# 128 unused bytes in front of two groups of stationary tiles in a one-core decoder trunk

## The chip, the cores and the metric

The kernel runs on one core of one Trainium2 chip. The metric is the device time of one execution in microseconds (us). Three timed runs of the kernel before took 2246.64, 2246.13 and 2247.63 us; their median is 2246.64 us.

## The reference

One layer of a hybrid decoder on 256 tokens of width 2048, in float32:

```python
x = x + 0.5 * _swiglu(_rmsnorm(x, ffn1_norm[l]), ffn1_w_gu[l], ffn1_w_down[l])
x = x + _token_mixing(_rmsnorm(x, mix_norm[l]), w_in[l], ...)
x = x + 0.5 * _swiglu(_rmsnorm(x, ffn2_norm[l]), ffn2_w_gu[l], ffn2_w_down[l])
```

`_swiglu` is `(silu(gate) * up) @ w_down` with a hidden width of 5632. The token mixing projects the normalised input once to 10,788 columns, runs three attention mixers on parts of it, multiplies each mixer's output by a branch matrix (256, 512 and 768 rows) and by a sigmoid gate, adds the three, and multiplies the sum by `w_out` (2048 x 2048). Almost all of the arithmetic is in the large matrix products, whose weights (some 400 MB) are each used once.

## The kernel before, in words

**The weight stream.** Every large product goes through `add_chunk` (L148): 256 tokens in two blocks `tb` of 128, times a chunk of 512 columns of a weight matrix (384 or 420 in part of the input projection). The weights are the moving operand, the activations the stationary one. A chunk is cut into units of two row blocks of 128. The weights are loaded by SyncE's queue, four row blocks at a time, into one of three `raw` tiles (L101). ScalarE rounds a unit into a `hi` tile (L111) and VectorE takes the rest into a `lo` tile (L112); there are four tiles of each. Then TensorE runs, for each row block `kt` and each token block, three matmuls into one PSUM bank:

```python
PE.matmul(o, lhs(kt, 0, tb), hi[:, k], start=kt == 0, stop=False)
PE.matmul(o, lhs(kt, 0, tb), lo[:, k], start=False, stop=False)
PE.matmul(o, lhs(kt, 1, tb), hi[:, k], start=False, stop=kt == nkt - 1)
```

These are lines 162, 163 and 164. Each loads its own 128 x 128 stationary operand first (the weight load, engine row PEld), so the first two load the same one twice. A full unit has 12 such matmuls. The order of the work is written out by hand in `stream` (L127): splits run three units ahead of the matmuls.

**The stationary tiles.** The activations, too, are kept in two parts, transposed: a tile `[128, n, 2, 256]` of 4-byte elements holds for row block `kt`, part `p` and token block `tb` the slice `[:, kt, p, tb*128:(tb+1)*128]`, which is 128 elements, 512 bytes in each partition, without gaps. Four tiles have this form, and each large product has one of them as its stationary operand:

- `xT` (L61, 16 row blocks): the normalised residual; for all of the gate and up products of both feed-forward parts and for the input projection.
- `ffn_midt` (L243, 24 row blocks; printed for both feed-forward parts under one name): for the down products. Each feed-forward part runs in two halves (L238), the first with 24 row blocks, the second with 20, each followed by four chunks of down product.
- `oT` (L406, 12 row blocks): the attention outputs, for the branch products.
- `mT` (L921, 16 row blocks): the merged branches, for the output projection.

**Where the tiles lie.** `xT` belongs to the pool `per`, which stays open to the end. The other three belong to pools that are opened on top of `per` when they are needed and closed again: `ffn_midt` is the first tile of its pool, `oT` the first of the pool `mix`, and `mT` the first of the pool `merge`, which lies behind `oT`. Tiles of a pool follow one another in the order of the program, each rounded up to a multiple of 32 bytes. In one partition `xT` takes 32,768 bytes; behind it come three `raw` (8,192 each), four `hi` and four `lo` (4,096 each), `ident`, `rows` and `cols` (512 each) and `dump` (2,048), all multiples of 512; then small tiles: `ssq` 32, `mhalf` 64, three `rstd` 32 each, three tables of 1,024, 1,024 and 3,072, `tabcmp` 512, `tabq12` 64, `tabq8`, `sink`, `nsink` and `gain` 32 each, and `w2` 1,024. What isn't a multiple of 512 among them adds up to 32 + 64 + 96 + 64 + 128 = 384. So `ffn_midt` and `oT` begin 100,736 bytes behind the start of `xT`, which is 196 times 512 and 384 more, and `mT` begins 24,576 bytes (48 times 512) behind `oT`. All `raw`, `hi` and `lo` tiles begin at the same offset modulo 512 as `xT`. `ffn_midt` begins 67,968 bytes behind the end of `xT`.

**Around it.** After a unit's matmuls, TensorE also runs short work that other lines have spawned: transposes of activations (L219, L269, L479, L701, L718, L937) and the attention products.

Of the kernel before, what the change touches and what calls it, by code (L numbers as in the profile page):

```python
# [9 lines left out]
F32 = mybir.dt.float32  # L10
# [6 lines left out]
T, D, FF = 256, 2048, 5632  # L17
# [15 lines left out]
class Ring:  # L33
    """Buffers handed out and given back in emission order."""

# [11 lines left out]
def hybrid_trunk_kernel(ctx, tc, x, ffn1_norm, ffn1_w_gu, ffn1_w_down, mix_norm, w_in, qk_gain, sinks, cmp_pos,  # L47
# [6 lines left out]
    per = ctx.enter_context(tc.tile_pool(name="per", bufs=1))  # L54
# [19 lines left out]

# [1 line left out]
    chains = []  # L76
# [17 lines left out]
    def add_load(src, nk, width, parts):  # L94
        """src: [128, nk, width] in DRAM; parts: [(k0, nk, mm, before, after)]"""
        li = len(loads)
        loads.append((src, nk, width))
        for k0, n, mm, before, after in parts:
            subs.append((li, k0, n, width, mm, before, after))
# [5 lines left out]
    def emit_split(si, k=None):  # L105
        """split of a unit, or of its k-th slice of 128 rows"""
        li, k0, n, width, *_ = subs[si]
        c = slice(0, n * width) if k is None else slice(k * width, (k + 1) * width)
        raw = raws[li % RAW_BUFS][:, k0 * width:(k0 + n) * width][:, c]
        hi, lo = his[si % SPLIT_BUFS][:, c], los[si % SPLIT_BUFS][:, c]  # L110
        ACT.activation(hi, raw, AF.Copy)  # L111
        DVE.tensor_tensor(lo, raw, hi.bitcast(F32), op=OP.subtract)  # L112
# [35 lines left out]
    def add_chunk(w, rows0, nkt, c0, width, lhs, evac, before=None, between=()):  # L148
        """out[tok, c0:c0+width] = lhs^T @ w[rows0:rows0+128*nkt, c0:c0+width]; lhs(kt, part, tb) -> [128, 128]."""
        bank = main[2 * (chunk_no[0] % 2):][:2]  # L150
        chunk_no[0] += 1
        wv = w[rows0:rows0 + 128 * nkt, c0:c0 + width].rearrange("(k p) c -> p k c", p=128)

        def mm_of(kt0, n):
            def mm(hi, lo):
                ks = [(k, tb) for k in range(n) for tb in range(2)]
                if kt0 + n == nkt:
                    ks.sort(key=lambda a: a[1])
                for k, tb in ks:
                    kt = kt0 + k  # L160
                    o = bank[tb][:, :width]
# [3 lines that stand above are left out]
            return mm  # L165

        step = SPLIT_KT if not loads else LOAD_KT
        for l0 in range(0, nkt, step):
            ln = min(step, nkt - l0)
            parts = []  # L170
            for s0 in range(0, ln, SPLIT_KT):
                sn = min(SPLIT_KT, ln - s0)
                last = l0 + s0 + sn == nkt
                first = l0 + s0 == 0
                parts.append((s0, sn, mm_of(l0 + s0, sn), before if first else None,
                              (lambda: evac(bank)) if last else None))
            add_load(wv[:, l0:l0 + ln], ln, width, parts)
            for args in between[l0 // step:l0 // step + 1]:
                add_load(*args)
# [14 lines left out]

# [1 line left out]
    def x_squares(j):  # L196
# [9 lines left out]
    def x_prep(norm, j):  # L206
        """The norm's share of columns 512j.., and their transposed two-part copy with the gain."""
        g0 = GAIN_ROW[norm]
# [25 lines left out]

# [1 line left out]
    def add_ffn(norm, w_gu, w_down, done):  # L236
# [3 lines left out]
        def open_pools():  # L240
            st["ctx"] = es = ExitStack()
            p = es.enter_context(tc.tile_pool(name=f"{norm}_mid", bufs=1, reuse_waits="tile"))
            st["mid"] = p.tile([128, 24, 2, T], F32R, name=f"{norm}_midt")  # L243
            st["sg"] = [p.tile([128, 512], F32, name=f"{norm}_sg{i}") for i in range(2)]
# [60 lines left out]

# [1 line left out]
    tabs = {}  # L307
# [8 lines left out]
    def row_cols(r0, r1, c0):  # L316
        """rows [0, r1) as columns, of which [r0, r1) are kept from column c0 on"""
        b = banks.take()
# [10 lines left out]

# [1 line left out]
    def build_tables():  # L331
        """Negated key distances, far below zero where a key is masked; constants of the heads' slopes."""
        p = tab_pool
# [63 lines left out]
    def add_mix(done):  # L397
# [6 lines left out]
        def open_mix():  # L404
            p = pool("mix")
            st["oT"] = p.tile([128, 12, 2, T], F32R, name="oT")  # L406
            p = pool("c", side="right")
# [26 lines left out]

        # per-head norms, transposes of queries and keys
        def raw_of(bank, width):
# [5 lines left out]
        def normed(bank, qr, c0, nh, const):  # L442
            """heads in qr[:, :, c0:c0+64nh]; bank is free to be written"""
            w = 64 * nh
# [24 lines left out]
        def transposed(jobs, finish):  # L469
            """jobs: (source of tb, evac); two jobs share a bank"""  # L470
            for a in range(0, len(jobs), 2):
# [21 lines left out]
        def q_evac(name, p0, h0, const):  # L493
            """six query heads h0.. to the pairs p0.."""
            def f(bank):
# [30 lines left out]
        def both_halves(dst, src, gain):  # L526
            """dst(g)[0:64] = dst(g)[64:128] = src[64g:64g+64] * gain"""
            for g in range(2):
# [25 lines left out]
        def ckv1_evac(bank):  # L554
            """k_cmp, v_cmp, k_slc"""
            qr = raw_of(bank, 384)
# [27 lines left out]
        def make_x(i):  # L584
            """cmp MLP input of keys (0) or values (1), two-part, on partitions (offset parity, d)"""
            X, Xs = st["X"], st["Xs"]
# [13 lines left out]
        def ckv2_evac(bank):  # L600
            """v_slc, k_win, v_win, gates"""
            for tb in range(2):
# [11 lines left out]
        def cmp_loads(i):  # L614
            """hidden layer of the cmp MLP: two loads, to be set between a chunk's"""
            wv = cmp_w1[0, i].rearrange("(k p) c -> p k c", p=128)
# [74 lines left out]

        # attention
        att = {"S": True, "O": True, "obs": {}}
# [15 lines left out]
        def apply_p(sb, blocks, pv):  # L709
            """blocks: (column of sb, keys); transposes them, then pv(pt, block index)"""  # L710
            while not (banks.free and att["O"] and st["pt"].free):
# [166 lines left out]
        def launcher():  # L878
            """starts attention units at a steady pace"""
            for name, marks, group in units:  # L880
# [15 lines left out]

        # gates, branch products, output projection
        def open_gates():
# [121 lines left out]

# [1 line left out]
    x2 = x[0].rearrange("(t p) d -> p t d", p=128)  # L1022
# [98 lines left out]
```

## Time and profile before

| what | value |
|---|---|
| median of three timed runs | 2246.64 us |
| span of the profiled execution (first to last instruction) | 2244.8 us |
| TensorE matmul busy (PE) | 2229.0 us, 99% of the span |
| TensorE weight load busy (PEld) | 1861.9 us, 83% |
| VectorE busy (DVE) | 1210.3 us, 54% |
| ScalarE busy (ACT) | 1019.4 us, 45% |
| moved by DMA | 404.82 MB, mean 180 GB/s |

The page gives the span of the profiled execution and no other time of it; the timed runs lie 1.3 to 2.8 us above that span. PE and PEld are two rows of one engine: the weight load of a matmul overlaps the matmul before it. Matmuls overlap one another too: a matmul is recorded from its start until its last result, which is longer than the distance from its start to the next one's start. That distance, read from the timeline, is called the step here.

### The profile page before, as it was taken

How to read it: one execution, taken by the hardware profiler on the slowest of the kernel's cores; microseconds unless marked ns; L12 is line 12 of the kernel's file. 1: busy time of each engine (PE TensorE's matmuls, PEld its weight loads, DVE VectorE, ACT ScalarE, POOL GpSimd, SP SyncE). 2: the span in 40 equal slices, each digit the busy share in tenths (PEclk: the TensorE clock that was granted, in tenths of full speed). 3: DMA queues.
4: the chain of work that ended last, by engine and by line, in shares of the span. 5: the costliest groups of instructions: out<-in, count | busy, mean ns of one | idle time of the engine just before them, and what ended most of it. 6: DMA issues, size and time to landing. Idle time of an engine off the chain costs nothing.

```text
span 2244.8 us, 26058 instructions
## 1 busy us (share of the span) xinstructions
PE 2229.0 (99%) x10417; PEld 1861.9 (83%) x10417; DVE 1210.3 (54%) x1618; ACT 1019.4 (45%) x1368; POOL 67.1 (3%) x83
## 2 busy tenths in 40 slices
PE   8999999999999999999999999999999999999999
PEld 7888888888888999998888888788888888888887
DVE  5755544455555576666555554555555544555553
ACT  5444433444444565555555444454444433444432
POOL 0000000000000121000001110100000000000000
PEclk9999999999999999999999999999999999999999
DMA  7555555555555564333345555555555555555553
GB/s 247 187 188 191 192 184 188 196 193 187 188 187 183 169 214 139 120 120 132 131 151 176 201 182 176 190 180 188 191 193 187 190 189 191 189 188 188 189 205 131
DMA packets 212626, 404.82 MB, mean 180 GB/s; under 512 B 7368, under 2 KB 36632, under 8 KB 212504
## 3 DMA queue, kind: packets, MB, share of 16 engines
q1 hardware_dynamic: 211696, 402.98, 52.9%
q8 instruction: 81, 1.33, 0.2%
q14 instruction: 41, 0.34, 0.0%
q10 hardware_dynamic: 808, 0.17, 0.0%
HBM read 401.03 MB, written 2.10 MB: 180 GB/s over the span
## 4 chain that ended last, share of the span: by engine, by line
PE 97%; DVE 1%; DMA 1%; POOL 0%; ACT 0%; issue 0%; SPq 0%; POOLq 0%; ACTq 0%
PE main L162 31%; PE main L164 30%; PE main L163 30%; PE misc L269 1%; PE misc L718 1%; PE misc L859 1%; PE misc L831 1%; POOL mg L958 0%; DVE lo L112 0%; PE misc L219 0%; PE misc L750 0%; PE misc L856 0%; ACT hi L111 0%; PE misc L832 0%; PE misc L769 0%
## 5 line engine op out<-in xcount | busy, mean ns | idle before, releaser
L112 DVE TENSOR_TENSOR lo<-raw,hi 128x1024 fp32r<-128x1024 f32 (+3 forms) x785 | 938.3, 1198 | 878.3 <-ACT hi L111 873.8
L111 ACT ACTIVATE hi<-raw 128x1024 fp32r<-128x1024 f32 (+3 forms) x785 | 808.1, 1032 | 922.4 <-PE main L164 906.1
L162 PE MATMUL main<-hi,xT 128*128 128x512 f32 (+1 forms) x2176 | 839.6, 386 | 3.1 <-ACT hi L111 3.1
L164 PE MATMUL main<-hi,xT 128*128 128x512 f32 (+1 forms) x2176 | 828.5, 381 | 0.0
L163 PE MATMUL main<-lo,xT 128*128 128x512 f32 (+1 forms) x2176 | 828.1, 381 | 0.1
L162 PEld LDWEIGHTS main<-hi,xT 128*128 128x128 f32 x2176 | 409.7, 188 | 81.7 <-issue 6.6
L164 PEld LDWEIGHTS main<-hi,xT 128*128 128x128 f32 x2176 | 409.0, 188 | 70.8
L163 PEld LDWEIGHTS main<-lo,xT 128*128 128x128 f32 x2176 | 409.3, 188 | 69.4 <-DVE lo L112 0.8
L162 PE MATMUL main<-hi,ffn_midt 128*128 128x512 f32 x704 | 278.4, 395 | 0.0
L164 PE MATMUL main<-hi,ffn_midt 128*128 128x512 f32 x704 | 277.9, 395 | 0.0
L163 PE MATMUL main<-lo,ffn_midt 128*128 128x512 f32 x704 | 277.8, 395 | 0.0
L164 PEld LDWEIGHTS main<-hi,ffn_midt 128*128 128x128 f32 x704 | 132.5, 188 | 31.2
L162 PEld LDWEIGHTS main<-hi,ffn_midt 128*128 128x128 f32 x704 | 132.5, 188 | 31.1
L163 PEld LDWEIGHTS main<-lo,ffn_midt 128*128 128x128 f32 x704 | 132.5, 188 | 30.9
L162 PE MATMUL main<-hi,mT 128*128 128x512 f32 x128 | 50.9, 398 | 0.0
L164 PE MATMUL main<-hi,mT 128*128 128x512 f32 x128 | 50.5, 395 | 0.0
L163 PE MATMUL main<-lo,mT 128*128 128x512 f32 x128 | 50.5, 394 | 0.0
L725 ACT ACTIVATE pt<-misc 128x256 f32<-128x256 f32 (+2 forms) x44 | 21.1, 490 | 58.8 <-PE misc L718 58.8
L190 DVE TENSOR_TENSOR ffn_midt<-misc,ffn_midt 128x512 fp32r<-128x512 f32 x44 | 28.3, 686 | 32.7 <-ACT ffn_midt L189 32.7
L189 ACT ACTIVATE ffn_midt<-misc 128x512 fp32r<-128x512 f32 x44 | 23.9, 596 | 46.4 <-PE misc L269 46.4
L845 ACT ACTIVATE sb<-sb,nm 128x32 f32<-128x32 f32 (+2 forms) x72 | 29.0, 403 | 28.9 <-DVE nm L839 28.9
L252 ACT ACTIVATE ffn_sg<-main,rstd_ffn 128x512 f32<-128x512 f32 x44 | 30.2, 688 | 22.8 <-PE main L164 20.4
(177 smaller groups left out, 1059.6 us busy)
## 6 DMA issues: line engine op xcount, KB each, us to landing
raw<-in_ffn_w_gu_dram SPq DMA_DIRECT2D x172, 1024.0 KB, 4.9
raw<-in_ffn_w_down_dram SPq DMA_DIRECT2D x88, 1024.0 KB, 5.0
raw<-in_w_in_dram SPq DMA_DIRECT2D x48, 1024.0 KB, 4.9
raw<-in_w_in_dram SPq DMA_DIRECT2D x44, 768.0 KB, 4.3
raw<-in_w_out_dram SPq DMA_DIRECT2D x16, 1024.0 KB, 5.0
raw<-in_ffn_w_gu_dram SPq DMA_DIRECT2D x8, 512.0 KB, 6.2
raw<-in_cmp_w_dram SPq DMA_DIRECT2D x4, 1024.0 KB, 5.8
raw<-in_w_branch_b_dram SPq DMA_DIRECT2D x4, 1024.0 KB, 5.0
```

Source lines behind the costliest of these rows:

```text
L111: ACT.activation(hi, raw, AF.Copy)
L112: DVE.tensor_tensor(lo, raw, hi.bitcast(F32), op=OP.subtract)
L162: PE.matmul(o, lhs(kt, 0, tb), hi[:, k], start=kt == 0, stop=False)
L163: PE.matmul(o, lhs(kt, 0, tb), lo[:, k], start=False, stop=False)
L164: PE.matmul(o, lhs(kt, 1, tb), hi[:, k], start=False, stop=kt == nkt - 1)
L189: ACT.activation(dst_hi, src, AF.Copy)
L190: DVE.tensor_tensor(dst_lo, src, dst_hi.bitcast(F32), op=OP.subtract)
L252: ACT.activation(st["sg"][tb], bank[tb], AF.Sigmoid, scale=r)
L269: PE.transpose(bv[:, k, tb * 128:(tb + 1) * 128], m[tb][:, c0:c0 + 128], ident)
L718: PE.transpose(place[i][:n], sb[:, c0:c0 + n], ident)
L831: PE.matmul(S0[:, :32 + nk], q, st["KC"][g][head_rows(h), :32 + nk], start=True, stop=True)
L845: ACT.activation(s, s, AF.Exp, bias=nm[:, 0, i:i + 1], scale=-1.0, accum_out=nm[:, 1, i:i + 1])
```

## The change

It allocates one tile of 32 float32 per partition (128 bytes), which nothing reads or writes, as the first tile of each feed-forward pool and of the pool `mix`. Everything behind it in these pools, and in the pools opened on top of them, begins 128 bytes further on: `ffn_midt`, `oT` and `mT` then begin 0 bytes modulo 512 from `xT`. The smaller tiles of these pools move by 128 bytes as well. No instruction is added, removed or reordered. The diff also takes out comments; its two other additions are

```diff
@@ def open_pools():
             p = es.enter_context(tc.tile_pool(name=f"{norm}_mid", bufs=1, reuse_waits="tile"))
+            p.tile([128, 32], F32, name=f"{norm}_shift")
             st["mid"] = p.tile([128, 24, 2, T], F32R, name=f"{norm}_midt")
@@ def open_mix():
             p = pool("mix")
+            p.tile([128, 32], F32, name="oT_shift")
             st["oT"] = p.tile([128, 12, 2, T], F32R, name="oT")
```

## Rows read from the trace of the kernel before

**Rows 1.** From the profile page, part 1 (busy time and share of the span of each engine) and part 4 (the chain of work that ended last, by engine).

```profile
PE 2229.0 (99%) x10417; PEld 1861.9 (83%) x10417; DVE 1210.3 (54%) x1618; ACT 1019.4 (45%) x1368; POOL 67.1 (3%) x83
...
PE 97%; DVE 1%; DMA 1%; POOL 0%; ACT 0%; issue 0%; SPq 0%; POOLq 0%; ACTq 0%
```

**Rows 2.** The waits, of TensorE and then of all engines: who waited for whom; us in total, times, longest us.

```profile
PE misc L937 <- POOL mg L958: 4.1, 4, 1.1
PE main L162 <- ACT hi L111: 3.1, 1, 3.1
PE misc L319 <- DMA rows<-in_ffn_norm_dram: 2.5, 1, 2.5
...
ACT hi L111 <- PE main L164: 906.1, 564, 1.9
DVE lo L112 <- ACT hi L111: 873.8, 708, 4.4
```

**Rows 3.** Groups of matmuls by line and shape: line, engine, operation, out<-moving,stationary, size of the stationary and of the moving operand, count | busy us, mean ns of one | idle before.

```profile
L162 PE MATMUL main<-hi,xT 128*128 128x512 f32 x1792 | 704.2, 393 | 3.1 <-ACT hi L111 3.1
L164 PE MATMUL main<-hi,xT 128*128 128x512 f32 x1792 | 698.8, 390 | 0.0
L163 PE MATMUL main<-lo,xT 128*128 128x512 f32 x1792 | 698.7, 390 | 0.0
L162 PE MATMUL main<-hi,ffn_midt 128*128 128x512 f32 x704 | 278.4, 395 | 0.0
L164 PE MATMUL main<-hi,ffn_midt 128*128 128x512 f32 x704 | 277.9, 395 | 0.0
L163 PE MATMUL main<-lo,ffn_midt 128*128 128x512 f32 x704 | 277.8, 395 | 0.0
...
L162 PE MATMUL main<-hi,mT 128*128 128x512 f32 x128 | 50.9, 398 | 0.0
...
L162 PE MATMUL main<-hi,oT 128*128 128x512 f32 x96 | 38.1, 397 | 0.0
```

**Rows 4.** The timeline of TensorE's matmuls (start us, duration us, engine, line, operation, operands, shapes, count): the first and the last of 38 that follow one another with `xT` as stationary operand.

```profile
539.53 0.39 PE L163 MATMUL main<-lo,xT 128*128 128x512 f32 x1
...
547.91 0.39 PE L164 MATMUL main<-hi,xT 128*128 128x512 f32 x1
```

**Rows 5.** The same view with `ffn_midt` as stationary operand, the first and the last of 37, 36, 36 and 37 that follow one another: one stretch from each of the four phases of down product.

```profile
340.14 0.40 PE L162 MATMUL main<-hi,ffn_midt 128*128 128x512 f32 x1
...
348.54 0.40 PE L162 MATMUL main<-hi,ffn_midt 128*128 128x512 f32 x1
...
688.71 0.40 PE L164 MATMUL main<-hi,ffn_midt 128*128 128x512 f32 x1
...
696.84 0.40 PE L163 MATMUL main<-lo,ffn_midt 128*128 128x512 f32 x1
...
1829.73 0.40 PE L162 MATMUL main<-hi,ffn_midt 128*128 128x512 f32 x1
...
1837.87 0.40 PE L164 MATMUL main<-hi,ffn_midt 128*128 128x512 f32 x1
...
2199.63 0.39 PE L162 MATMUL main<-hi,ffn_midt 128*128 128x512 f32 x1
...
2207.99 0.39 PE L162 MATMUL main<-hi,ffn_midt 128*128 128x512 f32 x1
```

**Rows 6.** The same view with `mT`, the first and the last of 34, and with `oT`, the first and the last of 10, that follow one another.

```profile
1472.16 0.39 PE L162 MATMUL main<-hi,mT 128*128 128x512 f32 x1
...
1479.84 0.39 PE L162 MATMUL main<-hi,mT 128*128 128x512 f32 x1
...
1325.25 0.40 PE L164 MATMUL main<-hi,oT 128*128 128x512 f32 x1
...
1327.35 0.40 PE L164 MATMUL main<-hi,oT 128*128 128x512 f32 x1
```

**Rows 7.** The same view where a phase of down product ends and `xT` takes over without a break: the first `xT` matmul, the eleventh and the nineteenth.

```profile
415.74 0.40 PE L162 MATMUL main<-hi,xT 128*128 128x512 f32 x1
...
418.05 0.39 PE L163 MATMUL main<-lo,xT 128*128 128x512 f32 x1
...
419.86 0.39 PE L162 MATMUL main<-hi,xT 128*128 128x512 f32 x1
```

**Rows 8.** The same view in the input projection, still with `xT`: the first and the last of 18 matmuls of 420 columns, and of 21 of 384 columns, that follow one another.

```profile
784.49 0.35 PE L164 MATMUL main<-hi,xT 128*128 128x420 f32 x1
...
787.76 0.35 PE L163 MATMUL main<-lo,xT 128*128 128x420 f32 x1
...
789.24 0.33 PE L162 MATMUL main<-hi,xT 128*128 128x384 f32 x1
...
792.71 0.33 PE L164 MATMUL main<-hi,xT 128*128 128x384 f32 x1
```

**Rows 9.** The instructions that read `hi`: weight loads (PEld) and matmuls with `xT` and `ffn_midt`, and the split on ScalarE; after the count: duration in ns min/median/max, first and last start.

```profile
L162 PEld LDWEIGHTS main<-hi,xT x2176: 186/188/330, 9.1 to 2127.4; 128*128 128x128 f32 x198
...
L162 PEld LDWEIGHTS main<-hi,ffn_midt x704: 187/188/192, 280.3 to 2239.8; 128*128 128x128 f32 x176
L162 PE MATMUL main<-hi,ffn_midt x704: 390/393/477, 280.5 to 2240.1; 128*128 128x512 f32 x176
```

**Rows 10.** Groups by line and shape of the two halves of the split of a full unit (columns as in rows 3).

```profile
L111 ACT ACTIVATE hi<-raw 128x1024 fp32r<-128x1024 f32 x687 | 726.2, 1059 | 892.5 <-PE main L164 880.6 <-DMA raw<-in_ffn_w_gu_dram 5.6 <-DMA raw<-in_w_branch_b_dram 3.4
...
L112 DVE TENSOR_TENSOR lo<-raw,hi 128x1024 fp32r<-128x1024 f32 x687 | 844.3, 1231 | 817.7 <-ACT hi L111 813.4 <-PE misc L750 1.3
```

**Rows 11.** Busy time in a stretch of down product and one of gate and up product (columns: stretch, its length, PE busy (count), PEld, DVE, ACT, POOL, granted TensorE clock, DMA share, GB/s).

```profile
530.00:550.00 20.00, 20.00 (x90) 16.56 (x89) 10.47 (x10) 7.79 (x8) 0.00 (x0) 1.00 0.62 211
360.00:380.00 20.00, 20.00 (x87) 16.13 (x86) 8.58 (x7) 7.82 (x8) 0.00 (x0) 1.00 0.55 179
```

## The prediction, made before the change was run

> **What bounds the kernel now.** I read the shares and the chain first, then TensorE's waits, then the groups of matmuls by stationary tile, and last the timeline, for steps. TensorE's matmul row is busy for 99% of the span and makes up 97% of the chain that ended last [rows 1]. Its own waits come to some 10 us in all, at the start and at four merges [rows 2]. The reader is to see in the other waits that the engines behind it wait for TensorE: ScalarE's split waits 906 us for a matmul to free a `hi` tile, and VectorE's waits for ScalarE's [rows 2]. A unit of 12 matmuls lasts about 12 x 0.227 = 2.7 us, while the two halves of its split take 1.06 and 1.23 us on two engines [rows 10]. So the time is the number of matmuls times the step from one to the next, and nothing but the step can be changed by an edit that adds and removes no instruction.
>
> The step isn't the same for all tiles. With `xT` it is (547.91 - 539.53) / 37 = 226.5 ns [rows 4]. With `ffn_midt` it is 8.40 / 36 = 233.3 ns in the first phase of down product, then 8.13 / 35 = 232.3, 8.14 / 35 = 232.6 and 8.36 / 36 = 232.2 ns [rows 5]. With `mT` it is 7.68 / 33 = 232.7 ns, with `oT` 2.10 / 9 = 233 ns [rows 6]. All have 512 moving columns, the same `hi` and `lo` tiles, and a full granted clock (1.00 in both stretches, the level of 2.4 GHz) [rows 11]. The splits beside them are the same too. The recorded durations tell the same more faintly, 390 against 395 ns [rows 3]. The weight load is no help: its median is 188 ns with either tile [rows 9]. What differs is the address of the stationary slice alone.
>
> **The change part by part.** It removes and adds no instruction, wait or transfer; the new tiles are neither read nor written. It has one effect to be priced: three stationary tiles come to `xT`'s offset modulo 512. If the offset sets the step, each matmul on them goes from its step to 226.5 ns. The counts are 3 x 704 = 2112 with `ffn_midt`, 3 x 128 = 384 with `mT`, 3 x 96 = 288 with `oT` [rows 3]. Each feed-forward part has 4 chunks x 24 row blocks x 2 x 3 = 576 matmuls in its first phase and 4 x 20 x 2 x 3 = 480 in its second.
>
> - first feed-forward: 576 x 6.8 ns = 3.9 us and 480 x 5.8 ns = 2.8 us
> - second feed-forward: 576 x 6.1 ns = 3.5 us and 480 x 5.7 ns = 2.7 us
> - `mT`: 384 x 6.2 ns = 2.4 us; `oT`, at `mT`'s difference since nine steps read to 10 ns are too coarse, 288 x 6.2 ns = 1.8 us
>
> The sum is 17.1 us. Not every matmul gets its full share: `xT` itself, after a down phase, takes 10 matmuls at (418.05 - 415.74) / 10 = 231 ns before it goes on at 1.81 / 8 = 226 ns [rows 7], and each break by transposes in an `mT` or `oT` chunk should cost such a run again. I take off 0.5 us and forecast a gain of 16.6 us.
>
> All of it should reach the end, since TensorE is the path. What could take it back is the split: with a unit of 12 x 226.5 ns = 2.72 us instead of 2.79 us, ScalarE and VectorE still have over a microsecond of slack per unit [rows 10], and the `xT` stretches already run at that rate with more DMA traffic (211 against 179 GB/s) [rows 11]. The four waits for the merge, 4.1 us, follow the end of a branch product and stay as they are [rows 2]. The other tiles that move (`ffn_sg`, `ffn_sil`, `ffn_m`, the attention tiles) are read and written by engines that wait for TensorE; I cost them at nothing, and an upper bound is little: even all 4.1 us of waits at the merges doubled would add 4 us.
>
> Bounds of the one unknown, the step on the moved tiles: below, `xT`'s 226.5 ns, the smallest settled step of any 512-column group; above, where the moved tiles would be worse off than now, the wider of the two steps that alternate in the first down phase, 0.24 us by the timeline's rounding. I take 226.5 ns.
>
> Why the offset rather than the place? `xT` alone doesn't guarantee a small step. With 384 columns its step is 3.47 / 20 = 173.5 ns, with 420 it is 3.27 / 17 = 192.4 ns [rows 8]. At 2.4 GHz the columns alone take 160 and 175 ns, so the rest is 13.5 and 17.4 ns; for 512 columns (213.3 ns) it is 13.2 ns with `xT` and 19 to 20 ns with the others. The same tile in the same place pays more as soon as the moving slices have a length (1,680 bytes) that is no multiple of 512. So the extra time follows how reads of the two operands fall against each other, and low address bits can do that. Also, `xT` entering with a large step settles within ten matmuls [rows 7], and `ffn_midt` never does over a whole phase [rows 5]. That is what a favourable and an unfavourable alignment would look like. It isn't proof: the moved tiles also lie 67,968 bytes and more behind `xT`'s end.
>
> A rule that speaks against the change: the Trainium skill, "TensorE: Matmul & The Clock Gate", section "Step-by-step: what each phase is for", says that TensorE reads the moving and the stationary operand through two independent ports, so that loading the next weights takes no read bandwidth from the running matmul. By it the step would not depend on the stationary address, and the sum would be 0. The rows above don't bear it out as far as the step goes: equal columns, 226.5 against 232 to 233 ns. The Trainium skill, "SBUF — State Buffer", section "Specifications (TRN2)", gives lines of 16 bytes; by lines alone a shift of 128 bytes changes nothing, again 0. No row here shows lines.
>
> **The rivals.**
>
> *The place counts, not the offset (or offsets modulo 128 or less).* Then the step stays at 232 to 233 ns, the change does nothing, and the time stays 2246.6 us. For it: all three slow tiles lie far behind `xT`, at many different distances, and the step is alike in all of them; the difference that the change removes and the difference in place can't be told apart by these rows. Against it: the 420-column step above, which place can't explain. In a sentence by itself: the two rules of the Trainium skill named above would have this outcome too.
>
> *In part.* The moved tiles settle only in some phases, as `ffn_midt` now has two patterns (233.3 ns in one phase, 232.2 to 232.6 in three). Half of the sum gives 2246.6 - 8.5 = 2238 us.
>
> *Slower: equal offsets are what costs.* `hi` and `lo` begin at `xT`'s offset modulo 512. If a stationary slice at the moving tile's offset reads against it, and `xT` is fast for its place in spite of this, the moved tiles get worse: at 240 ns the loss is 2784 x (240 - 232.7) = 20 us, 2267 us. It decides as soon as the step on `ffn_midt` is above 233.3 ns. For it: the steps of 0.23 and 0.24 us that take turns in the first down phase show that single steps of that size occur. Against it: the largest group with equal offsets, 5376 `xT` matmuls, has the smallest step.
>
> **How the numbers follow.** A measurement of this kernel can tell about 0.2%, 4.5 us. I give the full gain 0.46, the gain in part 0.06, no effect 0.39, and slower 0.09. So faster by over 0.2% is 0.52, within 0.2% is 0.39, slower is 0.09. The sum is made against the profiled execution, whose span is 2244.8 us: it would become 2228.2 us. The median of the timed runs lies 1.8 us above that span, so the predicted time is 2246.6 - 16.6 = 2230.0 us. Its own range is 2227 to 2236 us. The range for 8 in 10 has to take in no effect as well: from 2227 us to 2249 us (the slowest timed run, 2247.6, and a little for the moved small tiles); the slower case and what lies below are left out.
>
> **What would show it.** Right: the step on `ffn_midt`, `mT` and `oT` reads 226 to 227 ns in the timeline, their mean durations come to 390 ns, and `xT`'s rows stay. Place: those three steps stay at 232 to 233 ns and the median within 2 us. Slower: a step above 233.3 ns on them. The prediction is wrong, too, if `xT`'s own step changes or if waits of TensorE for a split appear in the down phases.

## The result, and the profile after

The changed kernel took 2230.44 us (median of four runs, 2229.94 to 2231.32) against 2246.39 us for the kernel before (2245.81 to 2247.63). The ratio is 0.9929, with a 95% interval of 0.9915 to 0.9943. The forecast was 2230.0 us.

The page's first part and the chain by engine, as in [rows 1]:

```profile
PE 2212.7 (99%) x10417; PEld 1859.6 (83%) x10417; DVE 1210.8 (54%) x1618; ACT 1019.1 (46%) x1368; POOL 66.9 (3%) x83
...
PE 95%; DVE 1%; issue 1%; DMA 1%; ACT 1%; POOL 1%; SPq 0%; ACTq 0%; POOLq 0%
```

The counts are those of [rows 1]: not an instruction more or less. PE's busy time fell by 2229.0 - 2212.7 = 16.3 us, the span by 2244.8 - 2228.5 = 16.3 us. VectorE, ScalarE and GpSimd are busy as long as before, to within half a microsecond. The waits, as in [rows 2]:

```profile
PE misc L939 <- POOL mg L960: 4.8, 4, 1.4
...
ACT hi L111 <- PE main L164: 889.2, 563, 1.9
DVE lo L112 <- ACT hi L111: 859.2, 709, 4.4
```

TensorE's own waits are the old ones. The splits wait 906.1 - 889.2 = 17 us less for TensorE, which is the same gain seen from the other side: they were early before and are a little less early now.

The groups of matmuls, as in [rows 3]:

```profile
L162 PE MATMUL main<-hi,xT 128*128 128x512 f32 x1792 | 704.5, 393 | 2.6 <-ACT hi L111 2.6
...
L162 PE MATMUL main<-hi,ffn_midt 128*128 128x512 f32 x704 | 274.6, 390 | 0.0
L164 PE MATMUL main<-hi,ffn_midt 128*128 128x512 f32 x704 | 274.0, 389 | 0.0
...
L162 PE MATMUL main<-hi,mT 128*128 128x512 f32 x128 | 50.3, 393 | 0.0
...
L162 PE MATMUL main<-hi,oT 128*128 128x512 f32 x96 | 37.5, 391 | 0.0
```

`ffn_midt`, `mT` and `oT` lost 5 to 6 ns of recorded duration each; `xT`'s group kept its mean of 393 ns. The steps say it more sharply. TensorE's timeline, the first and the last of 37 matmuls in a row with `xT`, then of 37, 36, 37 and 37 with `ffn_midt` (one stretch for each phase of down product), and of 33 with `mT`:

```profile
529.74 0.39 PE L162 MATMUL main<-hi,xT 128*128 128x512 f32 x1
...
537.90 0.39 PE L162 MATMUL main<-hi,xT 128*128 128x512 f32 x1
...
339.79 0.39 PE L163 MATMUL main<-lo,ffn_midt 128*128 128x512 f32 x1
...
347.95 0.39 PE L163 MATMUL main<-lo,ffn_midt 128*128 128x512 f32 x1
...
664.80 0.39 PE L163 MATMUL main<-lo,ffn_midt 128*128 128x512 f32 x1
...
672.78 0.39 PE L162 MATMUL main<-hi,ffn_midt 128*128 128x512 f32 x1
...
1811.78 0.39 PE L164 MATMUL main<-hi,ffn_midt 128*128 128x512 f32 x1
...
1819.94 0.39 PE L164 MATMUL main<-hi,ffn_midt 128*128 128x512 f32 x1
...
2179.66 0.39 PE L162 MATMUL main<-hi,ffn_midt 128*128 128x512 f32 x1
...
2187.82 0.39 PE L162 MATMUL main<-hi,ffn_midt 128*128 128x512 f32 x1
...
1464.72 0.39 PE L162 MATMUL main<-hi,mT 128*128 128x512 f32 x1
...
1471.98 0.39 PE L164 MATMUL main<-hi,mT 128*128 128x512 f32 x1
```

`xT`: 8.16 / 36 = 226.7 ns. `ffn_midt`: 8.16 / 36 = 226.7 ns in three phases and 7.98 / 35 = 228 ns in the second, whose stretch begins just after a break. `mT`: 7.26 / 32 = 226.9 ns. All four tiles now go at one pace, and the seam of [rows 7], where `xT` took over from `ffn_midt` and needed ten steps at 231 ns, is gone. The last matmul with `ffn_midt` and the seventh with `xT` after it:

```profile
411.41 0.39 PE L164 MATMUL main<-hi,ffn_midt 128*128 128x512 f32 x1
...
413.00 0.39 PE L162 MATMUL main<-hi,xT 128*128 128x512 f32 x1
```

That is 1.59 / 7 = 227 ns across the seam.

### The profile page after: what moved, and what is told of

Same layout as the page of the kernel before. It is cut to its first block, busy times and chain, and to the rows that moved or that the text cites. A ratio compares the mean times of both kernels' runs of the same rounds, so it can differ in the third digit from the quotient of the medians.

```text
span 2228.5 us, 26058 instructions
## 1 busy us (share of the span) xinstructions
PE 2212.7 (99%) x10417; PEld 1859.6 (83%) x10417; DVE 1210.8 (54%) x1618; ACT 1019.1 (46%) x1368; POOL 66.9 (3%) x83
## 4 chain that ended last, share of the span: by engine, by line
PE 95%; DVE 1%; issue 1%; DMA 1%; ACT 1%; POOL 1%; SPq 0%; ACTq 0%; POOLq 0%
PE main L162 30%; PE main L164 29%; PE main L163 29%; PE misc L270 1%; PE misc L720 1%; DVE lo L112 1%; PE misc L861 1%; ACT hi L111 1%; PE misc L833 1%; POOL mg L960 0%; DMA raw<-in_cmp_w_dram 0%; PE misc L219 0%; PE misc L752 0%; PE misc L858 0%; PE misc L834 0%
## 5 line engine op out<-in xcount | busy, mean ns | idle before, releaser
L111 ACT ACTIVATE hi<-raw 128x1024 fp32r<-128x1024 f32 (+3 forms) x785 | 808.1, 1032 | 907.2 <-PE main L164 889.2
L164 PE MATMUL main<-hi,xT 128*128 128x512 f32 (+1 forms) x2176 | 828.4, 381 | 0.0
L163 PE MATMUL main<-lo,xT 128*128 128x512 f32 (+1 forms) x2176 | 827.7, 380 | 0.0
L164 PEld LDWEIGHTS main<-hi,xT 128*128 128x128 f32 x2176 | 408.8, 188 | 71.1 <-DVE xT L193 0.2
L163 PEld LDWEIGHTS main<-lo,xT 128*128 128x128 f32 x2176 | 409.2, 188 | 69.3 <-DVE lo L112 0.8
L162 PE MATMUL main<-hi,ffn_midt 128*128 128x512 f32 x704 | 274.6, 390 | 0.0
L164 PE MATMUL main<-hi,ffn_midt 128*128 128x512 f32 x704 | 274.0, 389 | 0.0
L163 PE MATMUL main<-lo,ffn_midt 128*128 128x512 f32 x704 | 273.9, 389 | 0.0
L164 PEld LDWEIGHTS main<-hi,ffn_midt 128*128 128x128 f32 x704 | 132.1, 188 | 27.5
L163 PEld LDWEIGHTS main<-lo,ffn_midt 128*128 128x128 f32 x704 | 132.2, 188 | 27.4
L164 PE MATMUL main<-hi,mT 128*128 128x512 f32 x128 | 49.9, 390 | 0.0
L163 PE MATMUL main<-lo,mT 128*128 128x512 f32 x128 | 49.8, 389 | 0.0
```

## The experiments

The result confirms the steps, but not yet the reason. Moving three tiles by 128 bytes changes three things at once: their own address modulo 512, their distance from the moving tiles `hi` and `lo`, and their agreement with `xT`. *Distance* below is the start of a stationary tile less the start of the moving tiles, modulo 512: 0 for `xT` and 384 for the other three in the kernel before. The expectations also name starts in the partition (in the kernel before `xT`, `hi` and `lo` at 128 modulo 512, the other three at 0); no run shows these, and the argument needs only the differences. Each diff is against the kernel before, and where it says "pads of the change" it includes the two pads of 128 bytes. Line numbers move by a few lines in some of these kernels; L163 to L165 are then the three matmuls.

**All tiles moved together.** Pads of the change, and

```diff
+    per.tile([128, 96], F32, name="front_shift")
     x_sb = per.tile([128, 2, D], F32, name="x_sb")
```

> The changed kernel with 384 more unused bytes in front of all tiles: xT, hi, lo, ffn_midt, oT and mT all begin at 0 modulo 512 instead of all at 128, so every distance between a stationary and a moving tile is as in the changed kernel. Theory A (the distance between the stationary and the moving tile modulo 512 sets the step): steps of 226 to 227 ns everywhere, about 2230 us. Theory B (the stationary tile's own address modulo 512 sets it, 128 is good and 0 is bad): xT too goes to 232 ns and the others back to it; 8160 matmuls of 512 columns x 6 ns = 49 us more than the changed kernel, about 2279 us, some more from the 384-column matmuls.

2231.12 us, ratio 0.9934 (0.9918 to 0.9951). The timeline, the first and the last of 37 with `xT` and of 37 with `ffn_midt`, both beginning now, modulo 512, where `ffn_midt` began in the kernel before:

```profile
529.74 0.39 PE L164 MATMUL main<-lo,xT 128*128 128x512 f32 x1
...
537.90 0.39 PE L164 MATMUL main<-lo,xT 128*128 128x512 f32 x1
...
339.79 0.39 PE L165 MATMUL main<-hi,ffn_midt 128*128 128x512 f32 x1
...
347.95 0.39 PE L165 MATMUL main<-hi,ffn_midt 128*128 128x512 f32 x1
```

8.16 / 36 = 226.7 ns for both. `ffn_midt` sits at the very offset modulo 512 at which it was slow before, and is fast. Theory B, the stationary tile's own address, falls.

**Only the moving tiles moved.** No other pad:

```diff
+    per.tile([128, 32], F32, name="hi_shift")
     his = [per.tile([128, SPLIT_KT * 512], F32R, name=f"hi{i}") for i in range(SPLIT_BUFS)]
```

> 128 unused bytes in front of the four hi tiles and none elsewhere: all four stationary tiles begin at 128 modulo 512 exactly as in the changed kernel, but hi and lo begin at 256, so that every stationary tile has the distance (384 modulo 512) to the moving tiles that ffn_midt had in the kernel before. Theory A: all steps at 232 to 233 ns, xT's too; the kernel before plus 5376 xT matmuls x 6 ns = 32 us, about 2279 us, some more from the 384-column matmuls. Theory B: as the changed kernel, about 2230 us, all steps 226 to 227 ns.

2276.29 us, ratio 1.0136 (1.0121 to 1.0151): the four stationary tiles begin at one offset modulo 512, as the change wants it, at the very offset that they have in the changed kernel, and the kernel is 30 us slower than before. The first and the last of 36 with `xT` and of 36 with `ffn_midt`:

```profile
539.74 0.40 PE L164 MATMUL main<-lo,xT 128*128 128x512 f32 x1
...
547.87 0.40 PE L163 MATMUL main<-hi,xT 128*128 128x512 f32 x1
...
344.65 0.39 PE L163 MATMUL main<-hi,ffn_midt 128*128 128x512 f32 x1
...
352.78 0.39 PE L165 MATMUL main<-hi,ffn_midt 128*128 128x512 f32 x1
```

8.13 / 35 = 232.3 ns for either. `xT` hasn't moved at all and pays what `ffn_midt` paid; 5376 x (232.3 - 226.7) ns = 30 us, about the whole loss. So the distance between the two operands decides between the small step and the large one (theory A), and `xT`'s place is no advantage.

**Other distances.** Three kernels gave each stage a distance of its own, the first two by the size of the pads, the third by an offset within the tiles:

```diff
+            shift = {"ffn1": 256, "ffn2": 192}[norm]
+            if shift:
+                p.tile([128, shift // 4], F32, name=f"{norm}_shift")
             st["mid"] = p.tile([128, 24, 2, T], F32R, name=f"{norm}_midt")
...
+            p.tile([128, 16], F32, name="oT_shift")
...
+                    p.tile([128, 80], F32, name="mT_shift")
```

> Four other distances from the moving tiles, one per stage, xT as it was: ffn_midt of the first feed-forward at 128, of the second at 64, oT at 448 and mT at 256 modulo 512. Theory A with a period of 512: none of them as small as at 0, so 230 ns or more in all four. Theory A with a period of 256: mT alone at 226 to 227 ns. Theory B by the address modulo 256: mT (address 384) at 226 to 227 ns, ffn_midt of the first feed-forward (256) at 232. If only the old distance is bad, all four at 226 to 227 ns. Total between 2230 and 2250 us.

> Four more distances: ffn_midt of the first feed-forward at 320, of the second at 32, oT at 192, mT at 480 modulo 512. Theory A: if the step grows smoothly with the distance from 0, ffn_midt of the second feed-forward (32) and mT (480, that is -32) are nearest to 226.7 ns and the other two at 230 ns or more; if only exact multiples of a small block count, all four are alike at 230 ns or more. Theory B by the address modulo 256 says nothing on these, since none begins at 128. Total between 2230 and 2250 us.

> Four more distances: ffn_midt of the first feed-forward at 96, of the second at 160, oT at 16, mT at 240 modulo 512 (by an offset within the tiles, since tiles begin at multiples of 32). The runs before showed 0 and 256 alike (227 ns), 64 and 320 alike (233), 128 and 384 alike (232 to 233), 192 and 448 alike (229), 32 and 224 at 233. Theory A with a period of 256 and only a full match good: all four between 229 and 234 ns. If small misses were harmless, 16 and 240 (that is -16) would be at 227 to 229 ns.

They took 2242.24, 2246.51 and 2245.32 us (one run each). Two stretches of the first of them, 36 matmuls at distance 128 and 23 at distance 256; then 36 of the second at distance 320; then 35 of the third at distance 96:

```profile
344.77 0.40 PE L163 MATMUL main<-lo,ffn_midt 128*128 128x512 f32 x1
...
352.94 0.39 PE L162 MATMUL main<-hi,ffn_midt 128*128 128x512 f32 x1
...
1470.82 0.39 PE L164 MATMUL main<-hi,mT 128*128 128x512 f32 x1
...
1475.80 0.39 PE L162 MATMUL main<-hi,mT 128*128 128x512 f32 x1
```

```profile
344.82 0.39 PE L164 MATMUL main<-hi,ffn_midt 128*128 128x512 f32 x1
...
352.98 0.40 PE L163 MATMUL main<-lo,ffn_midt 128*128 128x512 f32 x1
```

```profile
344.81 0.40 PE L164 MATMUL main<-hi,ffn_midt 128*128 128x512 f32 x1
...
352.78 0.39 PE L162 MATMUL main<-hi,ffn_midt 128*128 128x512 f32 x1
```

All distances, each read in the same way from the timeline (start of the first and of the last matmul of a stretch without a break):

| distance | modulo 256 | stage | first, last start | steps | mean ns |
|---|---|---|---|---|---|
| 0 | 0 | `ffn_midt`, changed kernel | 339.79, 347.95 | 36 | 226.7 |
| 256 | 0 | `mT`, first map | 1470.82, 1475.80 | 22 | 226.4 |
| 16 | 16 | `oT`, third map | 1316.32, 1318.81 | 11 | 226 |
| 32 | 32 | `ffn_midt` 2nd, second map | 1837.76, 1845.92 | 35 | 233.1 |
| 64 | 64 | `ffn_midt` 2nd, first map | 1829.78, 1837.94 | 35 | 233.1 |
| 320 | 64 | `ffn_midt` 1st, second map | 344.82, 352.98 | 35 | 233.1 |
| 96 | 96 | `ffn_midt` 1st, third map | 344.81, 352.78 | 34 | 234.4 |
| 128 | 128 | `ffn_midt` 1st, first map | 344.77, 352.94 | 35 | 233.4 |
| 384 | 128 | `ffn_midt`, kernel before [rows 5] | 1829.73, 1837.87 | 35 | 232.6 |
| 160 | 160 | `ffn_midt` 2nd, third map | 1837.74, 1845.91 | 35 | 233.4 |
| 192 | 192 | `oT`, second map | 1318.51, 1320.80 | 10 | 229 |
| 448 | 192 | `oT`, first map | 1318.52, 1320.81 | 10 | 229 |
| 480 | 224 | `mT`, second map | 1477.79, 1481.99 | 18 | 233.3 |
| 240 | 240 | `mT`, third map | 1464.67, 1470.84 | 27 | 228.5 |
| 240 | 240 | `mT`, third map, the chunk before | 1441.10, 1448.58 | 33 | 226.7 |

The distances that are equal modulo 256 have equal steps: 0 and 256, 64 and 320, 192 and 448, and also 128 and 384 where the phase is the same (233.4 ns here, 233.3 ns in the first phase of [rows 5]). The period is 256 bytes, not the 512 by which the change was worked out. The small step isn't approached smoothly: 16 has it and 240 (that is -16) has it in some chunks, as the second expectation for the third map had it; 32 is far from it, and 192 lies in between for no reason that these runs show. I had expected 230 ns or more for 192 and 448; those were 1 ns off. No distance gave less than 226 to 227 ns. Nor does the distance fix the step to the nanosecond: in the kernel before, one distance and one tile gave 233.3 ns through the first phase and 232.2 to 232.6 ns through the others [rows 5], and the two rows for 240 are 1.8 ns apart in neighbouring chunks. What decides between two such values stays open.

**A pad of 384 instead of 128**, in both places, to have the period over long stretches and with an interval:

> 384 unused bytes in each of the two places instead of 128: ffn_midt, oT and mT begin at a distance of 256 bytes modulo 512 from the moving tiles. Period 256 (as mT in one stage has shown): all steps 226 to 227 ns and the changed kernel's time, 2230 to 2231 us. Period 512, with mT's stage an accident of its place: 232 ns on the long runs of ffn_midt, about 2243 us or more.

2231.27 us, ratio 0.9934 (0.9921 to 0.9946): the changed kernel's time within the interval, with 226.7 ns on `ffn_midt` in all but the second phase (226.9 ns). The period of 256 holds for the whole kernel.

**Only `lo` moved:**

```diff
+    per.tile([128, 32], F32, name="lo_shift")
     los = [per.tile([128, SPLIT_KT * 512], F32R, name=f"lo{i}") for i in range(SPLIT_BUFS)]
```

> 128 unused bytes in front of the four lo tiles alone: all stationary tiles and hi begin at 128 modulo 512, lo at 256. hi keeps the good distance 0, lo has the bad one (384). Theory A1 (each matmul pays by its own moving tile): the third of the steps in which lo streams (line 163) goes to 232 ns or more, the two thirds with hi stay at 227; 2230 + 2720 x 6 ns = 16 us, about 2246 us. Theory A2 (the small step needs all in line, since one bad matmul throws the next ones out): all three lines at 231 ns or more, about 2276 us as with hi and lo both moved. Theory B is already against the run with all moving tiles moved; by it 2230 us.

2274.57 us, ratio 1.0119 (1.0102 to 1.0136), with an unusual spread over its four runs, 2269.18 to 2282.86 us. The profiled run is the slowest of the four. Four matmuls that follow one another in it, with L164 the one that streams `lo`:

```profile
345.04 0.40 PE L163 MATMUL main<-hi,ffn_midt 128*128 128x512 f32 x1
345.28 0.40 PE L164 MATMUL main<-lo,ffn_midt 128*128 128x512 f32 x1
345.51 0.39 PE L165 MATMUL main<-hi,ffn_midt 128*128 128x512 f32 x1
345.74 0.40 PE L163 MATMUL main<-hi,ffn_midt 128*128 128x512 f32 x1
```

The steps are 0.24, 0.23 and 0.23 us; times rounded to 10 ns can't tell 0.227 from 0.233, but over a longer stretch from 345.04 to 352.98 us, 34 steps, the mean is 233.5 ns. Over all unbroken steps with `ffn_midt` in this run the means are 230.0 ns from L163 to L164, 235.7 from L164 to L165 and 234.2 from L165 to the next L163. None is the small step, as theory A2 has it (one line falls 1 ns short of the 231 ns that it named): two matmuls out of three at the good distance don't keep the small step, and by the medians one bad one per three costs about as much as all three (2274.57 against 2276.29 us). So the step isn't a sum of prices that each matmul pays for its own moving tile. One thing isn't told apart here: with `lo` alone moved, `lo` also lies at a distance of 128 bytes from `hi`, and no run has that without a misfit between `lo` and the stationary tiles.

**One part of the change alone**, the pad in front of `oT` taken out again:

> The change without its part in front of oT: ffn_midt at the moving tiles' offset, oT and mT as in the kernel before. If the gains of the parts add up, as they must where TensorE's step is all that changes: the kernel before less the ffn_midt terms alone, 3.9 + 2.8 + 3.5 + 2.7 = 12.9 us by the prediction's sum, so about 2233.3 us, with steps of 227 ns on ffn_midt and 232 ns on oT and mT. If the stages traded time with each other, anything else between 2230 and 2246 us.

2234.27 us, ratio 0.9947 (0.9934 to 0.9961). That is 11.6 us below the kernel before in the same runs (2245.89 us), where 12.9 us was expected; the interval reaches from 9 to 15 us. The steps are those expected, 226.7 ns on `ffn_midt` and 232.3 and 232.6 ns on `mT` and `oT` over all their unbroken stretches. The parts add up as far as this can tell.

**The 420-column chunk with aligned slices.** Pads of the change, and for width 420 the two row blocks of a unit 512 columns apart in `hi` and `lo`:

```diff
+        if width == 420:
+            raw = raw.rearrange("p (k c) -> p k c", c=width)
+            hi, lo = (t[si % SPLIT_BUFS].rearrange("p (k c) -> p k c", c=512)[:, :n, :width] for t in (his, los))
```

> The changed kernel with the two row blocks of a 420-column unit 512 columns apart in hi and lo instead of 420, so that both slices begin at the stationary tiles' offset modulo 256. If it was the second slice's offset (1,680 bytes on, 144 modulo 256) that kept the 420-column step at 192 to 193 ns, it falls to 175 + 13.3 = 188 ns. If it is the length of the stream, which is no multiple of 256 bytes, it stays at 192 to 193. The total changes by at most 0.5 us either way, so it is read from the steps.

2231.16 us (one run). The first and the last of 18 matmuls in a row, and of 23 a little later:

```profile
772.59 0.36 PE L169 MATMUL main<-lo,xT 128*128 128x420 f32 x1
...
775.84 0.35 PE L168 MATMUL main<-hi,xT 128*128 128x420 f32 x1
...
776.82 0.35 PE L169 MATMUL main<-lo,xT 128*128 128x420 f32 x1
...
781.07 0.35 PE L170 MATMUL main<-hi,xT 128*128 128x420 f32 x1
```

3.25 / 17 = 191.2 ns, then 4.25 / 22 = 193.2 ns. In the changed kernel 18 such matmuls, from 772.68 to 775.96 us, took 3.28 / 17 = 192.9 ns, and 23, from 777.52 to 781.75 us, 4.23 / 22 = 192.3 ns. One stretch gains 1.7 ns and the next loses 0.9; over all 93 steps between neighbours the means are 193.6 and 193.7 ns. So the step stays at 192 to 193 ns, the second expectation, and the offset of the second slice is worth nothing that can be read here. Nor does a bad distance make it longer: in the run in which `hi` and `lo` were moved, the steps of 420 columns have a mean of 193.0 ns, in the one with `lo` alone moved 191.6 ns. The length of the stream is what is left of the two causes that were weighed; no run gave another length that is no multiple of 256 bytes, so it is argued and not shown.

**A smaller stationary operand.** If the load of the next stationary operand held up the running stream byte for byte, a smaller load should cost less. In the down products only the first 64 tokens of each block of 128 are computed:

```diff
-                    o = bank[tb][:, :width]
+                    o = bank[tb][:lhs(kt, 0, tb).shape[-1], :width]
...
-                          lambda kt, p, tb: st["mid"][:, kt, p, tb * 128:(tb + 1) * 128],
+                          lambda kt, p, tb: st["mid"][:, kt, p, tb * 128:tb * 128 + 64],
```

> The down products of both feed-forward parts are computed for only the first 64 tokens of each block of 128 (the other 64 are left out), so that the stationary operand there has 64 columns, 256 bytes in a partition, instead of 128; the moving operand keeps its 512 columns. The first feed-forward keeps the bad distance 384, the second has the good one (0). Theory A says that the weight load's reads hold up the moving stream, so the extra over 213.3 ns should shrink with the load: by half, 213.3 + 6.7 = 220 ns in the second and about 213.3 + 9.5 = 223 ns in the first; about 2223 us in all. If the extra is a fixed cost of a matmul and the load only its victim: 226.7 and 232.9 ns as before, about 2240 us.

2241.93 us (one run). The weight load (PEld; after the count its duration in ns, min/median/max), then the first and the last of 37 matmuls of the first feed-forward part (distance 384) and of 36 of the second (distance 0):

```profile
L162 PEld LDWEIGHTS main<-hi,ffn_midt x704: 133/134/137, 280.7 to 2235.2; 128*64 128x64 f32 x176
```

```profile
344.64 0.39 PE L164 MATMUL main<-hi,ffn_midt 128*64 128x512 f32 x1
...
352.96 0.39 PE L164 MATMUL main<-hi,ffn_midt 128*64 128x512 f32 x1
...
1837.84 0.39 PE L164 MATMUL main<-hi,ffn_midt 128*64 128x512 f32 x1
...
1845.89 0.39 PE L163 MATMUL main<-lo,ffn_midt 128*64 128x512 f32 x1
```

The load fell from 188 ns [rows 9] to 134 ns, and the step at distance 0 *rose* from 226.7 to 8.05 / 35 = 230.0 ns. At distance 384 it *fell*, from 233.3 ns in the same phase [rows 5] to 8.32 / 36 = 231.1 ns. With the smaller operand the distance is worth about 1 ns in these stretches, where it was worth 6.6. Both expectations are missed. One more run took other sizes, both at distance 0:

> The down products are computed for only the first 96 tokens of each block of 128 in the first feed-forward and the first 32 in the second (the rest is left out); ffn_midt at the good distance 0 in both. With 64 tokens at that distance the step had been 230.0 ns, more than the 226.7 of 128, so a load that simply takes reads away from the stream (then 223 and 217 ns here) is against the run before. Theory A3 (the load's length shifts when the two operands' reads meet, and only some lengths fit): both between 226.7 and 235 ns, without order by size. A cost per byte after all: 96 below 226.7 and 32 well below it. Total about 2230 to 2242 us.

2241.81 us. The first and the last of 37 matmuls with 96 columns, and of 37 with 32:

```profile
344.62 0.39 PE L163 MATMUL main<-lo,ffn_midt 128*96 128x512 f32 x1
...
352.90 0.39 PE L163 MATMUL main<-lo,ffn_midt 128*96 128x512 f32 x1
...
1837.61 0.39 PE L163 MATMUL main<-lo,ffn_midt 128*32 128x512 f32 x1
...
1845.95 0.39 PE L163 MATMUL main<-lo,ffn_midt 128*32 128x512 f32 x1
```

8.28 / 36 = 230.0 ns and 8.34 / 36 = 231.7 ns. By the steps of 384 columns (173.5 ns, from [rows 8]) and of 512 a column of the stream takes (226.7 - 173.5) / 128 = 0.416 ns, which is one cycle at 2.4 GHz; 512 columns are 213.3 ns. At distance 0 the extra over that doesn't shrink with the load: it is 13.4 ns with 128 columns and 17 to 18 ns with 96, 64 and 32. Both steps lie in the wide range of theory A3, 226.7 to 235 ns, but not without order: at this distance the smaller load never had the smaller step. So "the load's reads hold up the stream, byte for byte" is against the runs. (The smaller operands also write fewer rows of the result; the runs don't separate that from the load.) What is shown is a condition: with stationary slices of 128 columns at a distance of a multiple of 256 bytes from `hi` and `lo`, streams of 384 or 512 columns run at their columns plus some 13.5 ns. Most other distances tried, other sizes of the stationary slice and streams of 420 columns cost 2 to 8 ns a matmul more; 16 bytes off cost between nothing and 1.8 ns in the table. What inside the engine makes the condition stays open.

## Why the prediction was right, point by point

**The bound** was right. Nothing but the step changed, and the span followed PE's busy time to a tenth of a microsecond.

**The sum** was right, and its terms too: with the steps read after, 576 x 6.6 + 480 x 5.6 + 576 x 5.9 + 480 x 5.5 ns = 12.5 us for `ffn_midt` (the settled step of 226.7 ns in all four phases), 384 x 5.8 ns = 2.2 us for `mT` and as many ns for 288 with `oT`, 1.7 us: together 16.4 us, for a measured 16.3 us of span. Added up over every matmul with these tiles in the two traces, the time from start to start fell by 12.4, 2.1 and 1.6 us, together 16 us. Without the deduction the forecast of 17.1 us was a little too large, because the step of `xT` read 226.5 ns from times rounded to 10 ns and is 226.7 ns; over the 2784 matmuls moved, 0.2 ns is 0.56 us. The deduction of 0.5 us was for another thing, settling, which is worth less (all unbroken steps with `mT` and `oT` have means of 227.0 and 226.9 ns, 0.2 us in all). That it made up for the rounding is luck. No cover was lost: TensorE waits no longer for a split than before. ([rows 11] lists the stretch of gate and up product first.)

**The reason** was right in kind and wrong in its period. Low address bits of one operand against the other, not the place, was the forecast's reading, and the two runs that moved all tiles or only the moving ones settle it. But the text spoke throughout of the offset modulo 512; the maps and the pad of 384 show that 256 is enough. And the offset of the stationary tiles alone, the one thing that the forecast priced, is half of the matter: with `hi` and `lo` moved away, four equal stationary offsets are worth nothing.

**The argument from the 420 columns** doesn't carry what was rested on it. That step does exceed the one of 384 and 512 columns, but it is the same with aligned slices (193.6 against 193.7 ns) and no longer at the bad distance (193.0 ns). So it is no evidence on address bits, and it was the prediction's main reason for the offset against the place. What was left for the offset was that `xT` settles and `ffn_midt` never does, and that the group with equal offsets has the smallest step; the rows before the change couldn't settle it, and 0.46 against 0.39 says as much. That the offset won is in part luck. That reads of the two operands fall against each other fits the dependence on distance but isn't shown; as a load that steals reads byte for byte it is against the runs with smaller loads.

**The rivals.** *The place* (0.39) is out: `xT` in its old place became slow, and the other tiles are fast in three different places (pads of 128 and 384 bytes, and all moved together). Its cousin, an offset modulo 128 or less, is out with it. *In part* didn't occur: no phase kept a large step. *Slower by equal offsets* is the reverse of what holds: equal offsets are the good case. The two rules of the Trainium skill that the prediction weighed would have had no gain. By the Trainium skill's rule on lines of 16 bytes ("SBUF — State Buffer", section "Specifications (TRN2)") 128 bytes wouldn't count, and here they did, by 16.3 us. By the Trainium skill's rule on independent ports ("TensorE: Matmul & The Clock Gate", section "Step-by-step: what each phase is for") the prediction had the step independent of the stationary address, and here it depends on where the two operands lie to each other (226.7 against 232 to 234 ns). The smaller loads don't speak clearly either way: one took 2.2 ns off the step at distance 384 and added 3.3 ns at distance 0.

## What to carry to other kernels

In a kernel that lives on back-to-back float32r matmuls, compare the steps of groups that differ only in their operands: a constant few nanoseconds between two stationary tiles of the same shape was 0.7% here, and 128 idle bytes removed it. Check the distance between stationary and moving tiles (a multiple of 256 bytes here), for every moving tile in the sequence, since one misfit in three cost about as much as all. Read a step from more than one stretch: two stretches of the same group differed by 2 ns here, as much as some of the effects that were looked for. A small tile of odd size, declared in front, shifts everything behind it, so such a gain can be lost or won by an edit that has nothing to do with it.

## What the runs showed of the hardware that was not expected

- The step depends on the start of the stationary slice relative to the moving slice modulo 256 bytes: 226.7 ns at 0, 256 and 16, 229 ns at 192, 226.7 or 228.5 ns at 240, and 232 to 234 ns at the others tried.
- A sequence in which one moving tile of two is at the wrong distance loses the small step everywhere (233.5 ns in the slowest of its runs), and its time varies from run to run by 13.7 us, where the other kernels that were run four times or more vary by less than 2 us.
- Stationary operands of 96, 64 and 32 columns at the good distance gave longer steps (230.0, 230.0, 231.7 ns) than 128 columns (226.7 ns), although the load of 64 took 54 ns less. At the bad distance 384 a stationary operand of 64 columns gave a shorter step than 128 (231.1 against 233.3 ns in the same phase).
- The step of 420-column streams had means of 191.6 to 194.3 ns in all runs, with no gain from the good distance or from aligned slices.
